# Two blocks of a feed-forward product pair by pair in single PSUM banks, their weights' parts made in an earlier stage

## The chip, the core and the metric

One core of a Trainium2 chip runs one launch of the kernel. The metric is the device time in microseconds. Five instruction streams work side by side and wait for each other by semaphores: TensorE (PE: matmuls and transposes), VectorE (DVE), ScalarE (ACT), GpSimd (POOL) and SyncE (SP), which here only issues DMAs. ScalarE issues DMAs too, in its own stream of instructions.

## What is computed

One layer of a diffusion backbone over 1152 tokens (1024 latent, 128 context) of width 1024, with a feed-forward width of 4096. The part after the token mixers is what the change touches:

```python
attn = _merge_heads(attend(_heads(q), k, v)) @ w_attn_proj
conv = (bg * _short_conv(cg * u, conv_w, conv_b)) @ w_conv_proj
mix = (jax.nn.sigmoid(ga) * attn + jax.nn.sigmoid(gc) * conv) @ w_o
x = _layer_norm(ALPHA * x + g1 * mix, ln1_g, ln1_b)
h = x * (1 + sc2) + sh2
f = jnp.square(jax.nn.relu(h @ w1 + b1)) @ w2 + b2
x = _layer_norm(ALPHA * x + g2 * f, ln2_g, ln2_b)
```

All is float32. An operand of a matmul is split into a high part (a cast) and a low part (the difference), and a product is three matmuls: high by high, high by low and low by high.

## The kernel before

The stages follow one another on TensorE: loading and modulation to 42 us of the span, attention to 380, the **mixers' stage** (gates, projections, convolution) to 758, the **output projection** by `w_o` to 887, the **first feed-forward product** to about 1300, the second to 1640, and the last layer norm.

*Mixers' stage.* Weights come through a `ring`: a raw tile `wr` by a DMA from SP (L94), `wh` as a cast on ScalarE (L109), `wl` as a difference on VectorE (L122). A chunk of 384 tokens takes one of six PSUM banks in turn. After each chunk `background(1)` takes one entry from the queue `bg`, which `gemv_rest` has filled with 109 entries: the rest of the modulation's product, VectorE's L741 on tiles `wmb`, in the pool `gp`.

*Output projection.* It runs in three passes, over 6, 9 and 3 pairs of a token tile and a half of the channels, 24 matmuls of 128x512 each (L1251 to L1253, tile `ps` in banks 4 to 7). A pass begins with the split of its own four weight tiles, which the code calls for during the last token tile of the pass before. Between matmuls `spend` hands out work from the list `todo`, by a budget in estimated us: the sums and moments of LN1 (`ln1_sum`, L985 to L989), its scaling (`ln1_apply`, L976 to L978 and L997 on `xk`), the *turns* (four transposes each of an `xk`, L1051, evacuated by ScalarE to `q`, L1061), and `combine`, which makes of the `q` of one **pair** (576 tokens, two times 288) the seven operands of a seven-product scheme in the manner of Strassen: high parts by ScalarE (L1069), low parts by VectorE (L1079), sums by VectorE (L1083). When `todo` is empty `spend` takes from `spare`: the two lists of `w1_ahead`. For each of the blocks 0 and 1 they load four raw tiles (L1150, `eh`), form the seven parts of the block's weights (sums L1134 in `S`, high L1158 in `ehT`, low L1162) and store them to DRAM as `w1d` (L1166 on SP), 14 units of two 128x512 tiles.

*First product.* There are 16 blocks `j`, each of seven products per pair, each product of 12 matmuls 128x288 (L1312 to L1314). Accumulators `dX`, `dV`, `dZ`, `dW` are two-bank tiles, one bank for each pair. Blocks 1 to 15 do both pairs at each product. Block 0 does all seven products of pair 0, then those of pair 1. During its first half the banks of pair 1 and the two of `dW` serve as four banks for the ten last turns, and during its second half `combine(1)` makes pair 1's operands; a product of pair 1 waits in the code until its part is made (`made <= k`). ScalarE copies accumulators out (`keep`, L1363), VectorE adds (`plus`, L1366); ReLU and square (L1320, L1321), differences (L1324), high and low parts (L1376, L1377) follow through the list `late`, and nine tiles per block go to DRAM by ScalarE's DMA issues (L1327, L1378, L1379). The weights' parts come from `w1d` by SP (L1191) for blocks 0 and 1, and are made in place (L1196, L1197) from block 2 on.

Of the kernel before, what the change touches and what calls it, by code (L numbers as in the profile page):

```python
# [144 lines left out]
def emit(nc, tc, ctx, aps, outs):  # L145
# [551 lines left out]
    gp = pool_on(s3, "gp", side="right")  # L697
# [16 lines left out]
    def gemv_rest():  # L714
# [3 lines left out]
        for g in range(8):  # L718
            st = {}

# [8 lines left out]
            def step(g=g, k=0, st=st):  # L729
                if k == 0:  # L730
                    start(g, st)
                    load(g, 0, st)
                if k + 1 < KB:
                    load(g, k + 1, st)
# [20 lines left out]
            def total(cond, g=g, st=st):  # L755
# [6 lines left out]
                dma(modd[cond:cond + 1, g * 512:(g + 1) * 512], ro)  # L762

# [26 lines left out]
        bg.append(fold)  # L790

# [29 lines left out]
    def attn_gate(j):  # L821
        w = ring.take()
        sg = tp.tile([P, NTOK + 4], F32, tag="t", name=f"sga{j}")
        for c in range(NCH):
            b = next_bank()
            run(chunk_mm(b, w, c))
            act(sg[:, csl(c)], b[:, :CH], AF.Sigmoid)
            background(1)
        sgs[j] = sg

    def attn_proj(j):
# [4 lines left out]
        for c in range(NCH):  # L836
# [3 lines left out]
            background(1)  # L840
# [52 lines left out]
    for j in range(6):  # L893
        w = ring.take()
        sg = tp.tile([P, NTOK + 4], F32, tag="t", name=f"sgc{j}")
        for c in range(NCH):
# [3 lines left out]
            background(1)  # L900
        w = ring.take(ahead=1 if j < 5 else 2)
        for c in range(NCH):
# [3 lines left out]
            background(1)  # L906
# [29 lines left out]

    HALVES = (slice(0, 512), slice(512, 1024))
# [4 lines left out]
    rawp = pool_on(sw, "rawp", side="right")  # L942
    wop = pool_on(swo, "wop", side="right")
    xkp = pool_on(sxk, "xkp", side="right")
    lnp = pool_on(sln, "lnp", side="right")
    tmp_n = [0]

    def tmp(pool, shape, tag, bufs, dtype=F32):
        tmp_n[0] += 1
        return pool.tile(shape, dtype, tag=tag, name=f"{tag}{tmp_n[0]}", bufs=bufs)  # L950

# [152 lines left out]
    WPARTS = ("A11", "S1", "S2", "A12", "S3", "S4", "A22")  # L1104
    NJ = NF // 2
    w1raw, w1sum, w1part = {}, {}, {}
    wtile = {}
# [8 lines left out]
    def w1_sum(u):  # L1116

        j, k = divmod(u, 7)
        if j >= NJ or (j, k) in w1sum:
            return  # L1120
        w1_load(j)
        a11, a12, a21, a22 = w1raw[j]
        name = WPARTS[k]
        if name[0] == "A":
            w1sum[j, k] = {"A11": a11, "A12": a12, "A22": a22}[name]
            return
        if name == "S4":
            t = w1sum[j, 2]
        else:
            t = tmp(wsp, [P, 512], "S1" if name == "S3" else name, 1)  # L1130
        w1sum[j, k] = t
        a, b, op = {"S1": (a21, a22, ALU.add), "S2": (w1sum.get((j, 1)), a11, ALU.subtract),
                    "S3": (a11, a21, ALU.subtract), "S4": (a12, w1sum.get((j, 2)), ALU.subtract)}[name]
        vec.tensor_tensor(out=t, in0=a, in1=b, op=op)  # L1134


    AHEAD = 2
    w1d = [dram.tile([P, 2, 512], F32, name=f"w1d{u}") for u in range(7 * AHEAD)]

    def ahead_tile(tag, dtype=F32):  # L1140
        tmp_n[0] += 1
        t = t1p.tile([P, 2, PT], dtype, tag=tag, name=f"e{tag}{tmp_n[0]}", bufs=1)
        return t.rearrange("p a b -> p (a b)")[:, :512]

    def w1_ahead(j):

        def load():
            w1raw[j] = [ahead_tile(f"h{n}") for n in ("11", "22", "12", "21")]
            for i in range(4):
                dma(w1raw[j][i], aps["w1"][j + i // 2 * NJ][:, HALVES[i % 2]])  # L1150

        st = {}

        def high(u):
            w1_sum(u)
            st[u] = (ahead_tile("hT2" if u % 2 else "hT4", F32R),
                     ahead_tile("hT3", F32R) if u % 2 else tmp(wsp, [P, 512], "lo2", 1, F32R))
            nc.scalar.copy(st[u][0], w1sum[j, u % 7])  # L1158

        def low(u):  # L1160
            hi, lo = st[u]
            vec.tensor_tensor(out=lo, in0=w1sum[j, u % 7], in1=f32(hi), op=ALU.subtract)  # L1162

        def keep(u):
            for i, x in enumerate(st.pop(u)):
                dma(w1d[u][:, i], f32(x))  # L1166

        out = [(0.0, load), (2.0, lambda: None)]
        units = range(7 * j, 7 * j + 7)
        for u in units:  # L1170
            out.append((0.0 if WPARTS[u % 7][0] == "A" else 0.7, lambda u=u: high(u)))
            if u > units[0]:
                out.append((0.0, lambda u=u: keep(u - 1)))
            out.append((1.6, lambda u=u: low(u)))
        out.append((1.0, lambda: keep(units[-1])))
        return out

    def w1_prep(u):
        j, k = divmod(u, 7)
        if j >= NJ:  # L1180
            return
        if u // 2 not in wtile:
            if u // 2 == 3:
                wtile[u // 2] = wo_last(u)
            else:
                wtile[u // 2] = [ringp.tile([P, 1024], F32R, tag=t, name=f"w1{t}{u}", bufs=3) for t in ("whi", "wlo")]
        hi, lo = (t[:, HALVES[u % 2]] for t in wtile[u // 2])
        w1part[u] = hi, lo
# [3 lines left out]
        else:  # L1192
            w1_sum(u)
            w1_sum(u + 1)
# [3 lines left out]
        if k == 6 and j + 1 >= AHEAD:  # L1198
            w1_load(j + 1)
# [20 lines left out]
    todo, spare = deque(), deque()  # L1220
# [13 lines left out]

    for j in range(AHEAD):
        spare.extend(w1_ahead(j))
# [44 lines left out]
    while spare:  # L1281
        spare.popleft()[1]()
# [4 lines left out]
    sln.close()  # L1287
    st0, sx1 = ExitStack(), ExitStack()
    t0p = pool_on(st0, "t0p")
    sp.close()  # L1290
# [3 lines left out]
    ps1 = pool_on(sp1, "ps1", space=bass.MemoryType.PSUM)  # L1294
# [5 lines left out]
    def dbank(tag, j):  # L1300
        return ps1.tile([P, 2, 512], F32, tag=tag, name=f"d{tag}{j}", bufs=1)

    def w1_mm(b, u, name, first, pairs):

        hi, lo = w1part[u]
        for p in pairs:
            o = b[:, p, :PT]
# [8 lines left out]
    def ht(tag, j):  # L1316
        return (t0p if tag[0] == "c" else t1p).tile([P, 2, PT], F32, tag=tag, name=f"{tag}_{j}", bufs=1)
# [8 lines left out]
    def spill(name, j, t):  # L1326
        nc.scalar.dma_start(hd[name, j], t)  # L1327

# [7 lines left out]
    both_p = slice(0, 2)  # L1336
    hip = None
# [17 lines left out]
    for j in range(NJ):  # L1355
        u = 7 * j
        bias = [b1c[:, j + i * NJ:j + i * NJ + 1] for i in range(2)]
        c1, c5, c2, c3 = (ht(t, j) for t in ("c1", "c5", "c2", "c3"))
        h = {n: ht("h" + n, j) for n in ("11", "22", "12", "21", "T2", "T3", "T4")}
        B = {}  # L1360

        def keep(out, b, f, sl=both_p):
            act(out[:, sl], b[:, sl, :PT], AF.Identity, bias=bias[f])  # L1363

        def plus(out, b, kept, sl=both_p):
            vec.tensor_tensor(out=out[:, sl], in0=b[:, sl, :PT], in1=kept[:, sl], op=ALU.add)  # L1366

        def finish(h=h, j=j):
            spill("T3", j, h["T3"])
            spill("T1", j, h["12"])  # L1370
            spill("T2", j, h["T2"])
            diff(h["T4"], h["21"], h["T2"])

            def parts(name, t):
                hi = tmp(hip, [P, 2, PT], "hi" + name, 1, F32R)
                nc.scalar.copy(hi, t)  # L1376
                vec.tensor_tensor(out=t.bitcast(F32R), in0=t, in1=f32(hi), op=ALU.subtract)  # L1377
                late.append(lambda: (nc.scalar.dma_start(hd[name, j][:, :, 0], f32(hi)),  # L1378
                                     nc.scalar.dma_start(hd[name, j][:, :, 1], t)))  # L1379
# [3 lines left out]


        for pairs in ((0,), (1,)) if j == 0 else ((0, 1),):
            sl = slice(pairs[0], pairs[-1] + 1)
            if pairs == (0,):
                store = list(segments(act_tiles(2), 0))
                todo.append((0.0, second_pair))
                B["X"], B["V"], B["W"] = dbank("X", 0), dbank("V", 0), dbank("W", "turn")  # L1390
                turn_banks.clear()
                turn_banks.extend(lambda n=n, i=i: B[n][:, i] for n, i in (("X", 1), ("V", 1), ("W", 0), ("W", 1)))
            for k, name in enumerate(WPARTS):
                new = {0: "X", 1: "V", 3: "Z", 6: "W"}.get(k)
                if new and pairs[0] == 0 and (j or k > 1):
                    while j == 0 and k == 6 and not made:
                        todo.popleft()[1]()
                    B[new] = dbank(new, j)
                if j:
                    w1_prep(u + k + 4)  # L1400
                while pairs == (1,) and made <= k:
                    todo.popleft()[1]()
                b = B["XVXZXVW"[k]]
                w1_mm(b, u + k, PARTS[k], bool(new), pairs)
                if k == 0:
                    keep(c1, b, 0, sl)
# [469 lines left out]
```

## Time and profile before

| | |
|---|---|
| time, median of 3 runs | 1688.82 us (1688.13 to 1691.61) |
| the profiled execution's own time | 1685.68 us |
| its span | 1683.9 us |
| PE, DVE, ACT, POOL busy | 95%, 61%, 43%, 12% |
| granted TensorE clock over the span | 0.979 |

The profiled execution is 3.1 us below the median, and its span 1.8 us below its own time. Shares are of the whole span; TensorE's missing 5% lies at the start and end, and between 758 and 953 us. In the page's 40 slices the granted clock, in tenths of full speed, reads `PEclk 9999999999999999999997899999999999999998`: it is short of 9 in two neighbouring slices in the middle (884 to 968 us) and in the last. In rows of the trace, "[1.49 <-ACT wh L109]" means that the engine stood idle for 1.49 us before the instruction and that ScalarE's line 109 writing `wh` released it. `SPq` and `ACTq` are the issues of DMAs, which don't count as busy time.

### The profile page before, as it was taken

How to read it: one execution, taken by the hardware profiler on the slowest of the kernel's cores; microseconds unless marked ns; L12 is line 12 of the kernel's file. 1: busy time of each engine (PE TensorE's matmuls, PEld its weight loads, DVE VectorE, ACT ScalarE, POOL GpSimd, SP SyncE). 2: the span in 40 equal slices, each digit the busy share in tenths (PEclk: the TensorE clock that was granted, in tenths of full speed). 3: DMA queues.
4: the chain of work that ended last, by engine and by line, in shares of the span. 5: the costliest groups of instructions: out<-in, count | busy, mean ns of one | idle time of the engine just before them, and what ended most of it. 6: DMA issues, size and time to landing. Idle time of an engine off the chain costs nothing.

```text
span 1683.9 us, 27308 instructions
## 1 busy us (share of the span) xinstructions
PE 1605.1 (95%) x10432; PEld 1543.4 (92%) x10432; DVE 1027.2 (61%) x1777; ACT 730.4 (43%) x1384; POOL 200.2 (12%) x214
## 2 busy tenths in 40 slices
PE   7999999999999999998886899999999999999995
PEld 5799999999999999996765799999999999999995
DVE  6568888654555565245563566666666457875666
ACT  5367777511122111132455465555655435454030
POOL 2145555100000001110000000000000121000002
PEclk9999999999999999999997899999999999999998
DMA  8332221222222222217534444454557898777792
GB/s 323 130 95 67 71 50 51 76 97 92 94 89 65 80 88 88 45 51 243 181 101 162 163 148 166 156 177 165 170 170 269 278 331 277 232 252 243 231 328 89
DMA packets 151819, 260.28 MB, mean 155 GB/s; under 512 B 40656, under 2 KB 58704, under 8 KB 151688
## 3 DMA queue, kind: packets, MB, share of 16 engines
q1 hardware_dynamic: 121320, 211.34, 38.9%
q10 hardware_dynamic: 30368, 47.20, 7.8%
q8 instruction: 82, 1.34, 0.3%
q14 instruction: 49, 0.40, 0.1%
HBM read 191.60 MB, written 66.88 MB: 154 GB/s over the span
## 4 chain that ended last, share of the span: by engine, by line
PE 77%; DVE 9%; ACT 6%; issue 3%; DMA 3%; POOL 0%; SPq 0%; POOLq 0%; ACTq 0%; DVEq 0%
PE ps L363 8%; PE ps L365 8%; PE ps L361 8%; PE pq L1565 6%; PE pq L1566 6%; PE pq L1567 6%; PE dX L1312 3%; PE dX L1314 3%; PE dX L1313 3%; PE ps L813 2%; PE ps L812 2%; PE ps L811 2%; PE dV L1313 2%; PE dV L1312 2%; PE dV L1314 2%
## 5 line engine op out<-in xcount | busy, mean ns | idle before, releaser
L365 PE MATMUL ps<-ahi,wl 128*128 128x384 f32 x864 | 292.5, 339 | 0.0
L361 PE MATMUL ps<-ahi,wh 128*128 128x384 f32 x864 | 292.5, 339 | 0.0
L363 PE MATMUL ps<-alo,wh 128*128 128x384 f32 x864 | 292.5, 339 | 0.0
L1565 PE MATMUL pq<-xh,vh 128*128 128x288 f32 x640 | 189.7, 296 | 4.5 <-ACT accc L1661 2.4
L1566 PE MATMUL pq<-xl,vh 128*128 128x288 f32 x640 | 188.8, 295 | 0.0
L1567 PE MATMUL pq<-xh,vl 128*128 128x288 f32 x640 | 188.2, 294 | 0.0
L361 PEld LDWEIGHTS ps<-ahi,wh 128*128 128x128 f32 x864 | 162.4, 188 | 1.5 <-issue 0.3
L363 PEld LDWEIGHTS ps<-alo,wh 128*128 128x128 f32 x864 | 162.5, 188 | 0.8
L365 PEld LDWEIGHTS ps<-ahi,wl 128*128 128x128 f32 x864 | 162.4, 188 | 0.0
L1565 PEld LDWEIGHTS pq<-xh,vh 128*128 128x128 f32 x640 | 119.9, 187 | 5.2 <-ACT accc L1661 2.6
L1567 PEld LDWEIGHTS pq<-xh,vl 128*128 128x128 f32 x640 | 120.6, 188 | 0.0
L1566 PEld LDWEIGHTS pq<-xl,vh 128*128 128x128 f32 x640 | 120.1, 188 | 0.0
L1532 DVE TENSOR_TENSOR xl<-hraw,xh 128x576 fp32r<-128x576 f32 x80 | 60.5, 756 | 78.3 <-ACT xh L1528 78.2
L122 DVE TENSOR_TENSOR wl<-wr,wh 128x1024 fp32r<-128x1024 f32 (+1 forms) x54 | 61.2, 1137 | 62.9 <-ACT wh L109 62.8
L741 DVE SCALAR_TENSOR_TENSOR acc<-wmb,sil,acc 128x512 f32<-128x512 f32 x112 | 81.6, 774 | 28.9 <-DMA wmb<-wmb 28.9
L1713 POOL TENSOR_TENSOR xm<-xm,ag 128x1024 f32<-128x1024 f32 x9 | 22.3, 2481 | 625.9 <-DMA xm<-xd 587.6
L1528 ACT CAST xh<-hraw 128x576 fp32r<-128x576 f32 x80 | 53.9, 673 | 97.5 <-issue 40.8
L1312 PE MATMUL dX<-hxahi,w1whi 128*128 128x288 f32 x248 | 74.6, 301 | 7.1 <-ACT q L1061 4.2
L1314 PE MATMUL dX<-hxahi,w1wlo 128*128 128x288 f32 x248 | 74.1, 299 | 0.1
L563 ACT ACTIVATE s<-s,st 128x512 f32<-128x512 f32 (+1 forms) x72 | 49.6, 688 | 51.5 <-DVE st L561 50.9
L1363 ACT ACTIVATE c<-dX,b1c 128x576 f32<-128x576 f32 (+1 forms) x51 | 36.4, 713 | 74.7 <-PE dX L1314 70.5
L109 ACT CAST wh<-wr 128x1024 fp32r<-128x1024 f32 (+1 forms) x62 | 57.7, 949 | 20.0 <-DMA wr<-wo 11.4
(354 smaller groups left out, 4377.2 us busy)
## 6 DMA issues: line engine op xcount, KB each, us to landing
w2r<-w SPq DMA_DIRECT2D x144, 256.0 KB
hraw<-hdT SPq DMA_DIRECT2D x60, 288.0 KB
wmb<-wmb SPq DMA_DIRECT2D x64, 256.0 KB
w1r<-w SPq DMA_DIRECT2D x28, 512.0 KB
hdB<-h ACTq DMA_DIRECT2D x48, 288.0 KB
hdT<-hT ACTq DMA_DIRECT2D x48, 288.0 KB
hraw<-hdB SPq DMA_DIRECT2D x44, 288.0 KB
mr<-wma SPq DMA_DIRECT2D x16, 512.0 KB
```

The lines of the kernel that those rows point to most:

```text
L122: engine.tensor_tensor(out=lo[:, :w], in0=self.raw.pop(i)[:, :w], in1=hi.bitcast(F32)[:, :w], op=ALU.subtract)
L361: mm(b[:, :CH], lhsT=hi[:, ws], rhs=a[0][:, kb, :], start=first and kb == 0, stop=False)
L363: mm(b[:, :CH], lhsT=hi[:, ws], rhs=a[1][:, kb, :], start=False, stop=False)
L365: mm(b[:, :CH], lhsT=lo[:, ws], rhs=a[0][:, kb, :], start=False, stop=last and kb == n - 1)
L741: vec.scalar_tensor_tensor(out=a, in0=t, scalar=sil[:, k, cond:cond + 1], in1=a, op0=ALU.mult, op1=ALU.add)
L1312: mm(o, lhsT=hi[:, ws], rhs=xh, start=first and kb == 0, stop=False, **kw)
L1313: mm(o, lhsT=hi[:, ws], rhs=xl, start=False, stop=False, **kw)
L1314: mm(o, lhsT=lo[:, ws], rhs=xh, start=False, stop=kb == 3, **kw)
L1532: vec.tensor_tensor(out=xl, in0=f32(x), in1=f32(xh), op=ALU.subtract)
L1565: mm(o, lhsT=hi[:, ws], rhs=xh[:, i], start=j == 0, stop=False)
L1566: mm(o, lhsT=hi[:, ws], rhs=xl[:, i], start=False, stop=False)
L1567: mm(o, lhsT=lo[:, ws], rhs=xh[:, i], start=False, stop=j == NJ - 1)
```

## The change

The making of the 14 units moves from the output projection to the mixers' stage: `w1_ahead` becomes the last entry of `bg`, opens a pool of its own (one buffer each for high, low, the four raw tiles and the sums) when the modulation's pool has been closed, and appends its 33 entries. `background(1)` becomes `background(1 + c % 2)`, four entries for three chunks, so that 142 entries find 156 places instead of 109 finding 117. The modulation's loads `wmb` are issued one further ahead. `spare` is gone, and `spend` deals only from `todo`.

In the first product both blocks 0 and 1 go pair by pair, in the order (0, pair 0), (1, pair 0), (0, pair 1), (1, pair 1), in single banks 0 to 3 of the pool that the output projection used. The turns use banks 6 and 7, two instead of four. Blocks 2 to 15 take two-bank tiles as before; their pool opens at block 2. The parts of blocks 0 and 1 are loaded from `w1d` twice, once for each pair. `keep`, `plus`, ReLU, square, differences, casts and stores of the two blocks work on one pair (128x288) instead of two (128x576). SP's DMA issues rise from 735 to 763, ScalarE's instructions from 1405 to 1447, VectorE's from 1703 to 1719; TensorE's stay at 10086.

```diff
@@ gemv_rest
         bg.append(fold)
+        bg.append(w1_ahead)
@@ new, before the mixers' loops
+    def w1_ahead():
+        sgp.close()
+        prep = pool_on(s3, "prep", side="right")
+        st = {}
+
+        def load(j):
+            w1raw[j] = [tmp(prep, [P, 512], f"r{i}", 1) for i in range(4)]
+            for i in range(4):
+                dma(w1raw[j][i], aps["w1"][j + i // 2 * NJ][:, HALVES[i % 2]])
+
+        def high(u):
+            if st:
+                keep(u - 1)
+            w1_sum(u, prep)
+            st[u] = tmp(prep, [P, 512], "hi", 1, F32R), tmp(prep, [P, 512], "lo", 1, F32R)
+            nc.scalar.copy(st[u][0], w1sum[u // 7, u % 7])
+
+        def low(u):
+            hi, lo = st[u]
+            vec.tensor_tensor(out=lo, in0=w1sum[u // 7, u % 7], in1=f32(hi), op=ALU.subtract)
+
+        def keep(u):
+            for i, x in enumerate(st.pop(u)):
+                dma(w1d[u][:, i], f32(x))
+
+        for j in range(AHEAD):
+            bg.append(lambda j=j: load(j))
+            for u in range(7 * j, 7 * j + 7):
+                bg.extend([lambda u=u: high(u), lambda u=u: low(u)])
+            bg.append(lambda: keep(max(st)))
@@ attn_gate, attn_proj, and the convolution's loops
-            background(1)
+            background(1 + c % 2)
@@ output projection
+    BLOCKS = [(j, (p,)) for p in range(2) for j in range(AHEAD)] + [(j, (0, 1)) for j in range(AHEAD, NJ)]
...
-        while todo and (room[0] >= 0 or not todo[0][0]) or spare and room[0] >= 0:
-            cost, fn = (todo or spare).popleft()
+        while todo and (room[0] >= 0 or not todo[0][0]):
+            cost, fn = todo.popleft()
...
-    for j in range(AHEAD):
-        spare.extend(w1_ahead(j))
@@ first product
-    sp.close()
+    turn_banks.clear()
+    turn_banks.extend(lambda i=i: bank(i) for i in (6, 7))
...
-    def dbank(tag, j):
+    def dbank(tag, j, pairs):
+
+        if len(pairs) == 1:
+            return bank("XVZW".index(tag)).rearrange("p (a b) -> p a b", a=1)
         return ps1.tile([P, 2, 512], F32, tag=tag, name=f"d{tag}{j}", bufs=1)
...
+    for n, (j, pairs) in enumerate(BLOCKS):
+        sl = slice(pairs[0], pairs[-1] + 1)
...
+            w1_prep(s_ + 4)
+            while pairs[-1] == 1 and made <= k and todo:
+                todo.popleft()[1]()
...
-                    spend(1.6)
+            if todo:
+                spend(1.3)
+            do_late()
```

On ScalarE, at the boundary between the first and the second pass of the output projection, the order before is this (`ehT` is a high part of `w1_ahead`, `wh` that of `w_o`'s tiles, `bag` the moments of LN1):

```order
L1158 CAST ehT_7974<-eh_7817 128x512
L1158 CAST ehT_8028<-eh_8011 128x512
L109 CAST wh_8041<-wr_7802 128x1024
L109 CAST wh_8053<-wr_7806 128x1024
L109 CAST wh_8065<-wr_8045 128x1024
L109 CAST wh3o_8082<-wr_8057 128x1024
L1158 CAST ehT_8119<-S_8117 128x512
L976 ACT_TABLE_LOAD
```

and of the changed kernel this:

```order
L109 CAST wh_7916<-wr_7788 128x1024
L109 CAST wh3o_7914<-wr_7820 128x1024
L109 CAST wh_8095<-wr_7920 128x1024
L109 CAST wh_8107<-wr_7924 128x1024
L109 CAST wh_8119<-wr_8099 128x1024
L109 CAST wh3o_8131<-wr_8111 128x1024
L1037 ACT_TABLE_LOAD
```

The casts of `w_o` follow each other with none of `w1_ahead` among them. On TensorE, where the seventh product of (block 0, pair 0) ends, stands before the first product of pair 1, on `hxahi_8882`, a part that `combine(1)` makes:

```order
L1313 MATMUL dW_9088<-hxs_8446,wh_8900 128x288
L1314 MATMUL dW_9088<-hxs_8445,wl_8901 128x288
L1312 MATMUL dX_8884<-hxahi_8882,w1whi_8687 128x288
L1313 MATMUL dX_8884<-hxahi_8882,w1whi_8687 128x288
L1314 MATMUL dX_8884<-hxahi_8882,w1wlo_8688 128x288
```

and in the changed kernel the first product of (block 1, pair 0), on `hxahi_8451`, the part of pair 0 that block 0 began with:

```order
L1313 MATMUL ps_9109<-hxs_8458,w1whi_8940 128x288
L1314 MATMUL ps_9109<-hxs_8457,w1wlo_8941 128x288
L1312 MATMUL ps_9142<-hxahi_8451,w1whi_8940 128x288
L1313 MATMUL ps_9142<-hxahi_8451,w1whi_8940 128x288
L1314 MATMUL ps_9142<-hxahi_8451,w1wlo_8941 128x288
```

Pair 1's first product has moved behind the 84 matmuls of (block 1, pair 0). On ScalarE in the mixers' stage, convolution gates (`sgc` is a gate's sigmoid, `hi` a high part of `w1_ahead`), the order before is

```order
L109 CAST wh_6904<-wr_6743 128x1024
L109 CAST wh_6965<-wr_6811 128x512
L899 ACTIVATE sgc_6971<-ps_6972 128x384
L899 ACTIVATE sgc_6971<-ps_7000 128x384
L203 CAST acch_0_7026<-acc_6781 128x512
L899 ACTIVATE sgc_6971<-ps_7030 128x384
```

and in the changed kernel

```order
L845 CAST hi_7060<-S_7058 128x512
L109 CAST wh_7063<-wr_6901 128x512
L968 ACTIVATE sgc_7069<-ps_7070 128x384
L968 ACTIVATE sgc_7069<-ps_7097 128x384
L845 CAST hi_7126<-S_6993 128x512
L968 ACTIVATE sgc_7069<-ps_7130 128x384
L845 CAST hi_7158<-r_6874 128x512
L109 CAST wh_7161<-wr_7002 128x1024
```

The 14 casts `hi` stand between the gates' sigmoids and the splits of the ring's weights.

## Rows read from the trace of the kernel before

**Rows 1.** Windows: stretch, length, busy PE, PEld, DVE, ACT, POOL, clock, DMA share, GB/s

```profile
380.00:760.00 380.00, 379.66 (x2178) 375.05 (x2177) 190.40 (x295) 81.42 (x139) 28.86 (x36) 1.00 0.25 78
890.00:929.00 39.00, 27.36 (x126) 25.46 (x126) 9.30 (x15) 22.93 (x59) 0.00 (x0) 0.65 0.36 137
```

**Rows 2.** Timeline, TensorE, second pass boundary: start, us, work, [idle before <-releaser]

```profile
797.97 0.49 PE L1251 MATMUL ps<-wh,ahi 128*128 128x512 f32 x1 [1.49 <-ACT wh L109]
799.23 0.80 PE L1252 MATMUL ps<-wl,ahi 128*128 128x512 f32 x1 [0.76 <-DVE wl L122]
800.25 0.63 PE L1251 MATMUL ps<-wh,ahi 128*128 128x512 f32 x1
803.88 0.49 PE L1251 MATMUL ps<-wh,ahi 128*128 128x512 f32 x1 [0.36 <-ACT wh L109]
805.14 0.50 PE L1252 MATMUL ps<-wl,ahi 128*128 128x512 f32 x1 [0.77 <-DVE wl L122]
808.32 0.50 PE L1252 MATMUL ps<-wl3o,ahi 128*128 128x512 f32 x1 [1.52 <-DVE wl3o L122]
```

**Rows 3.** Timelines of ScalarE and SyncE's queue around the same boundary

```profile
789.09 0.62 ACT L1158 CAST ehT<-eh 128x512 fp32r<-128x512 f32 x1 [0.94 <-DMA w1d<-ehT]
796.35 0.62 ACT L1158 CAST ehT<-eh 128x512 fp32r<-128x512 f32 x1 [6.64 <-DMA eh<-w]
796.88 1.99 ACT L109 CAST wh<-wr 128x1024 fp32r<-128x1024 f32 x2
786.15 0.32 SPq L1166 DMA_DIRECT2D w1d<-ehT  x1
```

**Rows 4.** Timelines of TensorE and VectorE, second pass: turns that wait

```profile
839.60 0.66 PE L1051 MATMUL ps<-ident,xk 128*128 128x128 f32 x4 [1.79 <-ACT xk L997]
847.01 0.66 PE L1051 MATMUL ps<-ident,xk 128*128 128x128 f32 x4 [0.80 <-ACT xk L997]
834.87 0.69 DVE L1162 TENSOR_TENSOR ehT<-S,ehT 128x512 fp32r<-128x512 f32 x1 [4.28 <-ACT ehT L1158]
```

**Rows 5.** Timeline, TensorE: end of output projection, blocks 0 and 1

```profile
886.61 0.39 PE L1253 MATMUL ps<-wh3o,alo 128*128 128x512 f32 x1
889.56 0.37 PE L1312 MATMUL dX<-hxahi,w1whi 128*128 128x288 f32 x1 [2.56 <-DMA w1whi<-w1d]
952.96 0.29 PE L1312 MATMUL dX<-hxahi,wh 128*128 128x288 f32 x1
974.91 0.29 PE L1312 MATMUL dW<-hxs,w1whi 128*128 128x288 f32 x1
```

**Rows 6.** TensorE's waits, 887 to 953: us in total, times, longest

```profile
PE dWturn L1051 <- ACT q L1061: 5.7, 2, 3.5
PE dX L1312 <- ACT q L1061: 4.2, 2, 2.1
```

**Rows 7.** Window of L1061 alone (turns' evacuations): busy of ACT, clock, DMA

```profile
887.00:953.00 66.00, 16.10 (x48) 0.72 0.39 136
```

**Rows 8.** Window of L1069 alone (casts of combined parts): busy of ACT, clock, DMA

```profile
887.00:953.00 66.00, 9.30 (x10) 0.72 0.39 136
```

**Rows 9.** Window of L997 alone (LN1's scaling): busy of ACT, clock, DMA

```profile
887.00:953.00 66.00, 2.69 (x4) 0.72 0.39 136
```

**Rows 10.** Groups by shape, ScalarE, 740 to 1320: busy us, mean ns, idle

```profile
L1363 ACT ACTIVATE c<-dX,b1c 128x576 f32<-128x576 f32 x45 | 33.4, 742 | 62.0 <-PE dX L1314 57.8 <-DMA hdB<-h 3.9
L1363 ACT ACTIVATE c<-dX,b1c 128x288 f32<-128x288 f32 x6 | 3.0, 497 | 12.7 <-PE dX L1314 12.7
```

**Rows 11.** ScalarE's queue, one issue of a store

```profile
947.98 0.34 ACTq L1327 DMA_DIRECT2D hdB<-h  x1
```

**Rows 12.** DMA, 885 to 960: GB/s in 40 slices

```profile
GB/s 204 199 317 404 399 392 401 393 391 319 17 0 0 0 0 0 0 0 0 0 9 0 0 0 0 44 312 203 155 303 106 0 0 0 157 189 205 349 412 131
```

**Rows 13.** Page: DMA queues (packets, MB, share of 16 engines)

```profile
q1 hardware_dynamic: 121320, 211.34, 38.9%
q10 hardware_dynamic: 30368, 47.20, 7.8%
```

More of the change, by code (lines that the diff above doesn't have):

```diff
@@ L717, in gemv_rest @@
         nc.scalar.copy(ones_r, ones)
-        for g in range(8):
-            st = {}
+        sts = [{} for _ in range(8)]
+        for g, st in enumerate(sts):
             def start(g=g, st=st):
@@ L762, in total @@
                 dma(modd[cond:cond + 1, g * 512:(g + 1) * 512], ro)
+                if cond and g + 1 < 8:
+                    load(g + 1, 0, sts[g + 1])
+                    load(g + 1, 1, sts[g + 1])
             for k in range(KB):
@@ L1137, in emit @@
[L1137 to L1188, printed above, removed]
+        j, k = BLOCKS[s_ // 7][0], s_ % 7
+        u = 7 * j + k
+        if s_ // 2 not in wtile:
+            wtile[s_ // 2] = [ringp.tile([P, 1024], F32R, tag=t, name=f"w1{t}{s_}", bufs=3) for t in ("whi", "wlo")]
@@ L1189, in w1_prep @@
+        hi, lo = (t[:, HALVES[s_ % 2]] for t in wtile[s_ // 2])
+        w1part[s_] = hi, lo
         if j < AHEAD:
@@ L1218, in emit @@
     seen, sums = {}, 0
[L1220 removed]
+    todo = deque()
     room = [0.0]
@@ L1353, in second_pair @@
             todo.extend(closures + [(0.0, count)])
-    for j in range(NJ):
-        u = 7 * j
-        bias = [b1c[:, j + i * NJ:j + i * NJ + 1] for i in range(2)]
[L1358 to L1371, printed above, removed]
+    store = list(segments(act_tiles(2), 0))
@@ new lines, in sums @@
+        def sums(h=h):
+            square(h["21"])
+            diff(h["T3"], h["22"], h["12"])
+            diff(h["12"], h["12"], h["11"])
+            diff(h["T2"], h["22"], h["12"])
+        for k in range(7):
+            s_ = 7 * n + k
+            new = {0: "X", 1: "V", 3: "Z", 6: "W"}.get(k)
+            if new:
+                B[new] = dbank(new, n, pairs)
+            w1_prep(s_ + 4)
+            while pairs[-1] == 1 and made <= k and todo:
+                todo.popleft()[1]()
+            b = B["XVXZXVW"[k]]
+            w1_mm(b, s_, PARTS[k], bool(new), pairs)
+            if k == 0:
+                keep(c1, b, 0)
+            elif k == 1:
+                keep(c5, b, 1)
+            elif k == 2:
+                keep(c2, b, 0)
+            elif k == 3:
+                plus(h["11"], b, c1)
+            elif k == 4:
+                keep(c3, b, 1)
+                plus(h["22"], b, c5)
+            elif k == 5:
+                plus(h["12"], b, c2)
+            elif not last:
+                plus(h["21"], b, c3)
+            if last and k == 6:
+                break
+            if todo:
+                spend(1.3)
+            do_late()
+            if k == 3:
+                after(lambda h=h: square(h["11"]))
+            elif k == 4:
+                after(lambda h=h, spill=spill: (square(h["22"]), spill("B11", h["11"])))
+            elif k == 5:
+                after(lambda h=h, spill=spill: (square(h["12"]), spill("B22", h["22"])))
+            elif k == 6:
+                after(sums)
+                after(lambda f=finish: late.append(f))
@@ L1577, in emit @@
     ps2 = pool_on(sp2, "ps2", space=bass.MemoryType.PSUM)
-    after(lambda h=h, j=j: (square(h["21"]), diff(h["T3"], h["22"], h["12"]), diff(h["12"], h["12"], h["11"]),
-                            diff(h["T2"], h["22"], h["12"])))
+    after(sums)
     after(finish)
@@ L1723, in emit @@
         if n == 8:
-            for stack in (swo, sw, st1):
+            for stack in (sw, st1):
                 stack.close()
```

187 lines of the change are left out of this document (73 added, 114 removed).

## The prediction

> **What bounds the kernel now.** I read first the table of stretches. In the mixers' stage TensorE is busy 379.66 of 380 us at full clock, with VectorE half idle and ScalarE four fifths idle [rows 1]: whatever small work goes there is hidden as long as it holds nobody up. From 758 us on it is different. [...] The timeline gives the frame: the output projection ends at 886.61 + 0.39 = 887.0 (call it T), block 0 begins at 889.56, block 1 at 952.96, and block 1's last four or so matmuls stand at 974.91 [rows 5]. So the two blocks end at about 975.3 = T + 88.3. Block 1, both pairs, takes 22.3 us, 168 matmuls at 0.133 us: two blocks without a hindrance are 44.7 us. Block 0's 63.4 us are the loss. [...]
>
> **Removing `w1_ahead` from the output projection.** The second pass begins late: idle 1.49 + 0.76 + 0.36 + 0.77 + 1.52 = 4.9 us, and behind the first two stand eight matmuls of 0.63 us [rows 2], where the usual one takes 0.39 [rows 5]: 8 x 0.24 = 1.9. Sum 6.8 us. The cause is one row up the chain: ScalarE's cast `ehT` at 796.35 waited 6.64 us for a load of `w1_ahead`, and `wh` stood behind it to 796.88 [rows 3]. In the new order nothing stands before these casts, so they begin when their buffers are free, some 4 to 5 us earlier. The third and fourth weight tile still come through two raw buffers, so the last wait of 1.5 and about another 1.5 stay: gain 3.8 (bounds 2 and 5). Two turns waited 1.79 + 0.80 for LN1's scaling [rows 4]; LN1 stood on VectorE behind a low part of `w1_ahead` that had itself waited 4.28 us [rows 4]. With that gone I take the whole 2.6 (bounds 0 and 2.6). The third pass begins with waits that LN1 and `combine(0)` cause on VectorE, not `w1_ahead`; their order changes by a few rows there, and I take nothing (bounds -1.5 and +1.5). Together T comes 6.4 us earlier (bounds 0.5 and 9).
>
> **Putting it into the mixers' stage.** 14 casts on ScalarE, 14 lows and 8 sums on VectorE, 8 loads and 28 stores on SP, some 14 x 0.62 + 22 x 0.69 = 24 us of work on two engines beside 380 us with at least 190 idle [rows 1]. It costs nothing as work. As a chain it could cost: there is one buffer for the high part, so a cast waits for the store before. A store was issued at 786.15 and let the next cast of its buffer go at 789.09 [rows 3], 2.9 us. One unit is then cast 0.62 + store 2.9 = 3.5 us, low parts likewise, while two entries of the queue come round in 1.5 chunks, 4.7 us at the mean of a gate's chunk (24 matmuls) and a projection's (12) at the stage's pace. Behind a late cast stand on ScalarE the gates' sigmoids and the ring's `wh`, and TensorE waits for those only when six banks are full. SP's loads of the ring stand behind stores that wait for a low part, with a whole weight tile of lead. I take 0. The bounds are 0 and 14 x 2.9 = 41 us, if every store held TensorE by its whole length; the value near 0 is nearest to the row of the stage itself, where VectorE's 190 us of similar entries left 0.34 us of idle TensorE.
>
> **The two blocks pair by pair.** The matmuls are the same. What changes is who waits. Before, pair 1's operands had to be made in the 39 us of pair 0's only half-block, and PE stood for the turns. Now 84 more matmuls of pair 0 lie between, and nobody but a turn needs pair 1 until (0, pair 1). So I ask how much ScalarE has to do between T and the end of the four half-blocks, because everything passes through it:
> - the ten turns' evacuations, 16.1 us [rows 7];
> - the casts of combined parts, 9.3 [rows 8], and LN1's last two scalings with their moments, 2.7 + 0.3 = 3.0 [rows 9];
> - a half-block's own work, 4 `keep`, 8 ReLU and square, 2 casts, at 0.497 us each at this width [rows 10]: 7.0, times four 27.8, less the 10 instructions of the last one that run beside block 2 (5.0): 22.8;
> - 9 stores for each of three half-blocks, 27 issues at 0.34 [rows 11], which the busy share hides: 9.2;
> - four casts of block 2's weights at 0.62 [rows 3]: 2.5.
>
> Sum 62.9 us. TensorE needs 44.7 and ten turns of 0.66 [rows 4], 51.3. ScalarE is the longer one. It won't run without a gap, since turns and accumulators still pass to and fro. Before, it was busy 22.93 of the 39 us [rows 1], 16 us of gaps; now TensorE always has a half-block of work that doesn't need ScalarE's newest result, but the turns have two banks instead of four. I take half, 8: the four half-blocks end at T + 71, bounds T + 63 and T + 79. Against T + 88.3 the gain is 17.3 (bounds 9 and 25). The first wait, 2.56 us for `w1whi` [rows 5], is inside T + 88.3, and I let it stand inside T + 71 as well.
>
> The rows show what the narrower work costs: `keep` takes 0.497 us at 288 and 0.742 at 576 [rows 10], so two halves cost 0.25 more than a whole, on 24 more instructions 6 us, and 18 more issues another 6, all of it in the sum above. [...]
>
> **Transfers.** 28 units of two 128x512 tiles are 14.7 MB, twice as much as before; with 1.75 blocks of stores (9 x 288 x 1024 bytes each, 4.6 MB), `xd` (1.6) and block 2's raw weights (1.0) it is 21.9 MB in some 70 us. Between 890 and 902 the trace shows 392 to 404 GB/s [rows 12]; at 400 that is 55 us. It is hidden, but not by much.
>
> **The sum.** 6.4 + 17.3 = 23.7 us. From the profiled execution's 1685.7 that is 1662; the median of the runs is 3.1 above that execution, so 1665. From block 2 on nothing changes. With all bounds together the forecast's own range is 1655 to 1679.
>
> **Rivals.**
> - *TensorE becomes the bound* (chance 0.09). If ScalarE's half-block work slips behind into block 2, where ScalarE has room, the end is TensorE's 51.3 + 1.5 = T + 53: gain 35 + 6.4, time 1647. For it: all of it but `keep` is put off by design. Against it: each of the ten turns and the parts of pair 1 are ScalarE's too, 28 us with LN1 before (0, pair 1) can run, and a full queue does not look ahead.
> - *The transfers set the pace* (0.17). SP's queue as a whole moves 211.34 MB in 38.9% of the span, 323 GB/s, and ScalarE's 47.20 MB in 7.8%, 359 [rows 13]. If ScalarE's issues wait for their places, the stores' 4.6 MB / 359 = 12.8 us come on top of its 71: T + 84, gain 4.3 + 6.4, time 1678. A sign of it is there already: `keep` waited once 3.9 us for `hdB<-h` [rows 10]. Against it: 21.9 MB at 323 are 68 us, still under 71. [...]
> - *The chain of stores stalls the mixers' stage* (0.08). One buffer, so each of 14 casts holds the sigmoids and `wh` behind it on ScalarE in front of a TensorE that is now never idle. It decides against the change from 24 us on, 1.7 of the 2.9 us of each unit: at 41 us the time is 1665 + 41 = 1706. Half of this (0.04) is slower, most of the rest within what can't be told. For it: in the output projection this same chain cost 6.64 us once. Against it: six banks of lead, and 3.5 us against 4.7.
>
> **How the numbers follow.** The forecast has 0.66. A measurement of this kernel tells about 0.2%, 3.4 us, from no change. Faster: 0.66 + 0.09 + 0.17 + 0.01 = 0.93; the same 0.03, slower 0.04. The range shall hold 8 in 10: forecast and transfers together have 0.83, so it reaches from below the forecast's fast end, 1652, to 1681, past the transfers' time; TensorE's 1647 and the stalled mixers lie outside.
>
> **What would show it.** Right: 380 to 758 us stays at 100% TensorE at full clock; the second pass begins with less than 3.5 us of idle time and no row of 0.63; no row of the mixers' stage waits for ScalarE; the four half-blocks end at T + 63 to T + 79 with ScalarE's queue, issues included, nearly without gaps, and the waits inside them are on `q`, `hxs` and on accumulators that `keep` has not freed. Wrong: idle TensorE before 758 behind `hi` or a sigmoid; waits of TensorE on `w1whi<-w1d`, or of ScalarE on `hd`, in the half-blocks (transfers); waits on `q` as long as before (the turns' two banks, which I have priced inside the 8 us of gaps); block 2 later than full speed because it inherits the last half-block's work.

## The result

| | before | after |
|---|---|---|
| median | 1689.72 us (4 runs) | 1670.72 us (4 runs, 1667.97 to 1671.68) |
| ratio, 95% interval | | 0.9884 [0.9867, 0.9902] |
| span of the profiled execution | 1683.9 us | 1669.9 us |

The changed kernel is 19 us faster (16.6 to 22.5 by the interval), and inside the range of the prediction, which said 1665. The two profiled executions differ by 14.0 us only: that of before is 4.0 below its median, that of after 1.0 above. What follows is read from these two and adds up to 14.

### The profile page after: what moved, and what is told of

It is laid out like the page before. It is cut to its first block, busy times and chain, and to the rows that moved or that the text cites. A ratio compares the mean times of both kernels' runs of the same rounds, so it can differ in the third digit from the quotient of the medians.

```text
span 1669.9 us, 27468 instructions
## 1 busy us (share of the span) xinstructions
PE 1599.8 (96%) x10432; PEld 1539.7 (92%) x10432; DVE 1026.0 (61%) x1793; ACT 734.8 (44%) x1408; POOL 201.4 (12%) x214
## 4 chain that ended last, share of the span: by engine, by line
PE 77%; DVE 8%; DMA 5%; ACT 5%; issue 3%; SPq 1%; POOL 0%; ACTq 0%; POOLq 0%; DVEq 0%
PE ps L363 8%; PE ps L365 8%; PE ps L361 7%; PE pq L1552 6%; PE pq L1553 6%; PE pq L1554 6%; PE dX L1312 3%; PE dX L1314 3%; PE dX L1313 3%; PE dV L1312 2%; PE dV L1314 2%; PE dV L1313 2%; PE ps L880 2%; PE ps L881 2%; PE ps L882 2%
## 5 line engine op out<-in xcount | busy, mean ns | idle before, releaser
L1699 POOL TENSOR_TENSOR xm<-xm,ag 128x1024 f32<-128x1024 f32 x9 | 22.5, 2497 | 607.6 <-DMA w2r<-w 545.0
L743 DVE SCALAR_TENSOR_TENSOR acc<-wmb,sil,acc 128x512 f32<-128x512 f32 x112 | 78.2, 748 | 12.3 <-DMA wmb<-wmb 12.2
L1312 PE MATMUL dX<-hxahi,w1whi 128*128 128x288 f32 x224 | 67.5, 301 | 5.5 <-DVE h L1367 5.5
L1314 PE MATMUL dX<-hxahi,w1wlo 128*128 128x288 f32 x224 | 67.0, 299 | 0.0
L881 PE MATMUL ps<-acl,wh 128*128 128x384 f32 x192 | 64.2, 334 | 0.0
```

Of the source, the lines that this page charges most:

```text
L881: mm(b[:, :CH], lhsT=hi[:, ws], rhs=parts[kb][1][:, cs_], start=False, stop=False)
L1312: mm(o, lhsT=hi[:, ws], rhs=xh, start=first and kb == 0, stop=False, **kw)
L1314: mm(o, lhsT=lo[:, ws], rhs=xh, start=False, stop=kb == 3, **kw)
```

## The profile after

T again is the end of the output projection. The stretches of the changed kernel, to be laid beside [rows 1] (columns as there):

```profile
380.00:760.00 380.00, 378.56 (x2173) 374.14 (x2172) 193.47 (x307) 85.49 (x145) 27.80 (x34) 1.00 0.33 101
881.00:920.00 39.00, 29.95 (x174) 28.00 (x172) 16.60 (x25) 31.12 (x76) 0.00 (x0) 0.82 0.63 216
920.00:940.00 20.00, 15.96 (x116) 15.34 (x115) 12.84 (x19) 9.63 (x19) 0.00 (x0) 1.00 0.99 330
940.00:953.00 13.00, 12.69 (x92) 11.99 (x90) 4.03 (x9) 5.90 (x14) 0.00 (x0) 1.00 1.02 360
953.00:962.00 9.00, 3.55 (x15) 3.55 (x16) 6.83 (x13) 5.82 (x12) 0.00 (x0) 0.74 0.24 85
```

The mixers' stage still looks full, but 380 us hold 1.4 us of idle TensorE where there were 0.3. At the start of the first product ScalarE is busy 31.12 of 39 us, where it was 22.93, and TensorE's mean clock is 0.82 where it was 0.65 (this stretch begins at T, that of before 3 us behind its T). From 920 to 953 the DMA engines are full: a share of 0.99 to 1.02 at 330 to 360 GB/s. And in 953 to 962 TensorE has only 3.55 us of work in 9.

The boundaries of the output projection's second and third pass, in TensorE's timeline:

```profile
804.27 0.50 PE L1248 MATMUL ps<-wh,ahi 128*128 128x512 f32 x1 [0.23 <-ACT wh L109]
805.53 0.50 PE L1249 MATMUL ps<-wl,ahi 128*128 128x512 f32 x1 [0.76 <-DVE wl L122]
807.73 0.50 PE L1249 MATMUL ps<-wl3o,ahi 128*128 128x512 f32 x1 [0.54 <-DVE wl3o L122]
...
859.47 0.50 PE L1248 MATMUL ps<-wh,ahi 128*128 128x512 f32 x1 [1.75 <-ACT wh L109]
860.73 0.50 PE L1249 MATMUL ps<-wl,ahi 128*128 128x512 f32 x1 [0.76 <-DVE wl L122]
865.46 0.50 PE L1248 MATMUL ps<-wh,ahi 128*128 128x512 f32 x1 [0.46 <-ACT wh L109]
```

The first three rows are the second pass, to be laid beside [rows 2]: its first two waits are gone, 0.23 + 0.76 + 0.54 = 1.5 us remain of 4.9, and no matmul of 0.63 us stands there any more. The last three are the third pass. Its wait for `wl` is 0.76, where the kernel before had

```profile
866.62 0.80 PE L1252 MATMUL ps<-wl,ahi 128*128 128x512 f32 x1 [4.08 <-DVE wl L122]
```

but the wait for `wh` just before has grown from 0.85 to 1.75. From the last matmul of the second pass to T the third takes 24.1 us instead of 26.2.

The two blocks, same engine, as in [rows 5]: the last matmul of the output projection, the first of the first product, the last of the four half-blocks and the first of block 2.

```profile
881.02 0.40 PE L1250 MATMUL ps<-wh3o,alo 128*128 128x512 f32 x1
881.26 0.29 PE L1312 MATMUL ps<-hxahi,w1whi 128*128 128x288 f32 x1
...
952.68 0.29 PE L1314 MATMUL ps<-hxs,w1wlo 128*128 128x288 f32 x1
958.45 0.61 PE L1312 MATMUL dX<-hxahi,w1whi 128*128 128x288 f32 x1 [5.48 <-DVE h L1367]
958.86 0.44 PE L1313 MATMUL dX<-hxahi,w1whi 128*128 128x288 f32 x1
```

T is 881.42; the first product begins at once; the four half-blocks end at 952.8 = T + 71.4; block 2 begins only at 958.45, after 5.48 us of waiting, and then at the lower clock (0.24 us from one matmul to the next, 22 of the first 24). What it waits for is seen on the other engines, in one row of SP's queue, one of ScalarE and two of VectorE:

```profile
947.40 14.58 SPq L1173 DMA_DIRECT2D w1r<-w  x3
953.66 0.62 ACT L1195 CAST w1whi<-w1r 128x512 fp32r<-128x512 f32 x1 [3.53 <-DMA w1r<-w]
955.16 0.69 DVE L824 TENSOR_TENSOR S<-w1r 128x512 f32<-128x512 f32 x1 [4.54 <-DMA w1r<-w]
957.94 0.45 DVE L1367 TENSOR_TENSOR h<-ps,c 128x288 f32<-128x288 f32 x1
```

The loads of block 2's raw weights `w1r` are issued from 947.4 on, behind the second round of `w1d` loads; ScalarE and VectorE wait 3.53 and 4.54 us for them, and the additions (L1367) that empty the last half-block's banks stand on VectorE behind the weights' sums (L824). So `dX`, which takes two of those banks, waits for an addition whose product had long been finished (the last matmul of all four half-blocks ended at 952.97, the addition began at 957.94).

Where the 14.0 us of the two spans come from, by TensorE's timeline. Its marks are the first 128x384 matmul of the attention ("start" below), the first of the output projection, T, and the first of blocks 2 and 3. The start, which the change doesn't touch, lies between 83.4 and 85.1 in all twelve profiles and is 0.8 us later here:

| stage | before | after | gain |
|---|---|---|---|
| start of attention | 83.4 | 84.3 | -0.8 |
| from there to the output projection | 674.6 | 678.6 | -4.0 |
| output projection | 128.9 | 118.5 | +10.4 |
| T to the end of the two blocks | 88.3 | 71.4 | +16.9 |
| block 2, beyond 22.4 us | 0.0 | 8.2 | -8.2 |
| the rest | | | -0.3 |

## The experiments

On two chips, with the kernel before beside them each time (medians 1687.6 to 1688.4): e5 to e8 on one, the others on another. e5, e6 and e7 ran once each, so they have no interval. "Half-blocks to" is the time from T to the end of the four half-blocks, and to block 2's first matmul where TensorE waited between the two; for the kernel before and e3_only_ahead it is that of blocks 0 and 1. "Both stages" is the time from the output projection's first matmul to the same end. Both are read from one profile of each kernel.

| kernel | us | ratio [95%] | half-blocks to | both stages |
|---|---|---|---|---|
| before | 1687.6 to 1688.4 | | T + 88.3 | 217.2 |
| r_after | 1671.25 | 0.9893 [0.9876, 0.9909] | T + 69.2, block 2 at T + 75.3 | 189.7 |
| e3_only_ahead | 1671.01 | 0.9900 [0.9886, 0.9915] | T + 76.3 | 196.8 |
| e4_only_blocks | 1680.15 | 0.9953 [0.9936, 0.9969] | T + 74.1, block 2 at T + 79.6 | 204.0 |
| e1_early_raw | 1664.37 | 0.9856 [0.9840, 0.9872] | T + 69.4 | 190.0 |
| e2_pace | 1667.21 | 0.9877 [0.9859, 0.9896] | T + 72.8, block 2 at T + 78.4 | 191.3 |
| e8_both | 1660.37 | 0.9831 [0.9817, 0.9844] | T + 70.6 | 191.2 |
| e9_pool_stores | 1658.11 | 0.9815 [0.9801, 0.9830] | T + 66.5 | 187.0 |
| e5_no_square | 1661.82 | | T + 71.2 | 188.6 |
| e6_half_loads | 1661.13 | | T + 64.7 | 185.4 |
| e7_four_banks | 1661.15 | | T + 68.7 | 187.8 |

**The changed kernel beside the others.** Same file, on the chip of e1 to e4 and e9.

> The changed kernel again, on the chip of the other experiments: 0.986 to 0.991 of the kernel before, so that e1_early_raw's 0.9856 and e8_both's 0.9831 stand against a value measured beside them.

0.9893, where the first measurement had 0.9884; its output projection took 120.5 us and its half-blocks T + 69.2, where the profile above has 118.5 and T + 71.4. The two trade some 2 us from one execution to the next, so a difference of that size in one stage says nothing. Their sum trades less: 189.9 above, and 189.7 to 191.3 in the table for the four kernels that should hardly differ there (r_after, e1_early_raw, e2_pace, e8_both).

**Each half alone.** First half: the 14 units in the mixers' stage, blocks as before (the loops of the first product, the four turn banks and the order of block 0 are those of the kernel before).

```diff
+        bg.append(w1_ahead)
...
-            background(1)
+            background(1 + c % 2)
...
-        while todo and (room[0] >= 0 or not todo[0][0]) or spare and room[0] >= 0:
+        while todo and (room[0] >= 0 or not todo[0][0]):
```

> The kernel before (1689.7 us) with only the first half of the change: the 14 units are made in the mixers' stage, the blocks of the first product stay as they were. Theory: the mixers' stage gives back about 4 us, the output projection gains about 10.5, the first wait of 2.56 us on w1whi goes: in sum 7 to 9, 1681 to 1683, and the first product from its first matmul on takes the 399 us of before. Rival: the output projection's gain at its third pass (about 2.6) belongs to the other half of the change: 1683 to 1686.

More than either expectation: 0.9900, 17 us, nearly all of the whole change. The mixers' stage lost its 3 to 4 us, as said; the output projection took 120.5 us, 8.5 less, where 10.5 were expected. What was not foreseen is the first product:

```profile
881.55 0.40 PE L1249 MATMUL ps<-wh3o,alo 128*128 128x512 f32 x1
881.78 0.29 PE L1306 MATMUL dX<-hxahi,w1whi 128*128 128x288 f32 x1
...
958.27 0.29 PE L1306 MATMUL dX<-hxahi,w1whi 128*128 128x288 f32 x1
```

881.95 to 958.27 are 76.3 us for blocks 0 and 1 in their old order, 12.0 less than in the kernel before. The rows account for most of it: the first wait (2.56) is gone; TensorE's waits in the two blocks sum to 16.6 us instead of 21.9, that one included; some 52 matmuls instead of 99 run at the lower clock, 47 x 0.11 = 5.2 us. One unit of `w1_ahead` had been left for the end of the output projection (before: a cast on ScalarE at 888.08, its lows and stores behind it), ahead of the last tile's LN1, and with it the last turns came 2.5 us later after T. That this small delay and the lower clock explain all 12 us was argued from rows, not tried apart.

Second half alone: the order of half-blocks, the units made in the output projection.

```diff
+    for j in range(AHEAD):
+        spare.extend(w1_ahead(j))
...
-        bg.append(w1_ahead)
...
-            background(1 + c % 2)
+            background(1)
```

> The changed kernel with only its second half: two blocks pair by pair, and the 14 units made in the output projection as before. Theory: the halves are independent, so this one gains what the first product gained, 8 to 10 us: 1680 to 1682; the output projection takes its 129 us. Rival: the units' stores, the second loads and the half-blocks' stores meet after the output projection and the half-blocks get longer than T + 77: 1684 to 1688.

1680.15, 7.5 us: the theory's time. The output projection takes 129.9 us, the half-blocks end at T + 74.1 and block 2 waits as in the changed kernel. The two halves alone give 17 and 8 us, the whole change 17 to 19: they are not independent, since both shorten the same stretch behind T. On top of the first half the second shows nothing in the time: 1671.01 without it, 1671.25 with it. The half-blocks end 5 to 7 us sooner with it, and block 2's wait and lower clock take that back.

**Block 2's raw weights loaded earlier.**

```diff
             w1_prep(s_ + 4)
+            if s_ == 7:
+                w1_load(AHEAD)
```

> The changed kernel (1670.7 us), with block 2's two raw weight tiles loaded when (block 1, pair 0) begins instead of late in (block 1, pair 1). Theory: the 5.48 us for which TensorE waited at block 2's first matmul, and the 22 matmuls at the lower clock behind it (some 2.5 us), come from these loads standing behind the second round of w1d loads: the wait is under 1 us and the time 1662 to 1664. Rival: the wait is the handing over of single banks to two-bank tiles, which needs the last half-block's additions whatever the loads do: the wait stays above 4 us and the time within 1669 to 1672.

```profile
883.26 0.40 PE L1250 MATMUL ps<-wh3o,alo 128*128 128x512 f32 x1
...
953.09 0.29 PE L1312 MATMUL dX<-hxahi,w1whi 128*128 128x288 f32 x1
```

No wait at block 2's first matmul, at 953.09 = T + 69.4, and it runs at full clock (0.29); 1664.37, 6.9 us below the changed kernel on the same chip and 0.4 above the theory's 1662 to 1664. With the weights there, the banks' handing over shows no wait.

**A total no longer in the call of its cut.** Among the modulation's entries in the queue, a *cut* splits a sum of VectorE into high and low part (`acch`, `accl`), and the *total* behind it adds them up over the partitions by two matmuls of TensorE. A cut now returns `True` and ends the call:

```diff
+        owed[0] += n
+        while owed[0] > 0 and (bg or later):
+            owed[0] -= 1
+            if (bg or later).popleft()():
+                break
...
                 st["hl"] = hi, lo
+                return True
```

> The changed kernel, where a call of the mixers' background queue ends after a cut, so that the total which needs it comes one chunk later; what is left of the call is made up at the next. Theory: the 4 us that the mixers' stage lost come from totals of the modulation right behind their cut (waits of 1.08, 0.34 and 1.01 us), not from the chain of stores: the waits on acch and accl are under 0.5 us in sum, and the time is 2 to 3 us shorter, 1668. Rival: the 14 units' casts and stores cost the 4 us: no change, 1670 to 1672.

TensorE's waits from 320 us to the output projection, first of the changed kernel, then of this one:

```profile
PE ps L761 <- DVE accl L204: 1.4, 2, 1.0
PE ps L760 <- ACT acch L203: 1.1, 1, 1.1
PE ps L365 <- DVE wl L122: 0.9, 2, 0.5
```

```profile
PE ps L365 <- DVE wl L122: 0.2, 1, 0.2
```

The waits on the modulation's totals are gone, the output projection begins at 758.0 instead of 762.9 (0.8 of that is the earlier start of the attention), and the median is 4.0 us below r_after's. The intervals of the two ratios overlap, so the time alone wouldn't decide; the stage does. From the start of the attention to the output projection it takes 674.6 us here, 674.8 in e8_both and 674.7 in e9_pool_stores, which have the same edit, as in the kernel before (674.6), and 677.4 to 678.6 in the seven profiles with the units there and without the edit. The chain of stores never reached TensorE: before seven of the 14 casts ScalarE stood idle until a store `w1d<-hi` had landed, 23.1 us in sum, but from 650 us on, where `w1_ahead` has its places, no TensorE row of the changed kernel waits.

**Both together.**

> e1_early_raw and e2_pace together. Theory: two losses in different stages add: 1664.4 - 3 = 1661, a ratio of 0.983 to 0.985 to the kernel before.

1660.37, ratio 0.9831, against 1664.4 - 4.0 = 1660.4: they add.

**What sets the length of the half-blocks.** e1_early_raw without ReLU and square of blocks 0 and 1 (so that part of the activations is left out):

```diff
+        sq = square if n >= 2 * AHEAD else lambda t: None
```

> e1_early_raw, where its four half-blocks end at T + 69.4 (T is the end of the output projection). ReLU and square of blocks 0 and 1 are left out, some 26 ScalarE instructions of 0.45 us before that point, 12 us. Theory: ScalarE sets the length of the half-blocks, so they end at T + 58 to T + 62. Rival: turns, TensorE and the transfers set it: T + 67 or more.

```profile
879.29 0.40 PE L1250 MATMUL ps<-wh3o,alo 128*128 128x512 f32 x1
...
950.91 0.29 PE L1312 MATMUL dX<-hxahi,w1whi 128*128 128x288 f32 x1
```

950.91 - 879.69 = 71.2: not a microsecond shorter, and 1.4 us by both stages, where the theory wanted 7 to 11. The theory that ScalarE's work is the bound falls. The second round of loads halved (the low parts of pair 1's weights are not read):

```diff
-            for i, x in enumerate((hi, lo)):
+            for i, x in enumerate((hi, lo) if s_ < 7 * AHEAD else (hi,)):
...
+            if s_ >= 7 * AHEAD:
+                w1part[s_] = hi, hi
```

> e1_early_raw, where the second round of w1d loads, for pair 1, brings only the high parts (the low operand of these products is the high part again): 3.7 MB less, some 9 us of transfers. Theory (ScalarE is the bound, the transfers add waits only in the third and fourth half-block): the ScalarE waits on landings of w1d there go, the half-blocks end at T + 65 to T + 68. Rival (transfers set the pace): T + 61 to T + 64. If the transfers are hidden: T + 69.

```profile
882.00 0.40 PE L1252 MATMUL ps<-wh3o,alo 128*128 128x512 f32 x1
...
947.06 0.29 PE L1314 MATMUL dX<-hxahi,w1whi 128*128 128x288 f32 x1
```

947.06 - 882.40 = 64.7, 4.7 us less than e1_early_raw (4.6 by both stages), between the theory's span and the rival's. Four turn banks instead of two:

```diff
-    turn_banks.extend(lambda i=i: bank(i) for i in (6, 7))
+    turn_banks.extend(lambda i=i: bank(i) for i in (4, 5, 6, 7))
```

> e1_early_raw with four turn banks instead of two (4 to 7). Theory: the 3.8 us for which turns waited on ScalarE's evacuations are ScalarE's time in another place, so the half-blocks end within 1.5 us of T + 69.4. Rival: the two banks hold TensorE up: T + 65 to T + 67.

T + 68.7, within the 1.5 us (2.2 us less by both stages, in this one execution). So neither ScalarE's work nor, as far as one execution tells, the banks, but something with the transfers. The whole times of the three, 1661.1 to 1661.8, don't tell them apart. In the changed kernel's trace it is this: an issue of ScalarE's queue, its next instruction, and the matmul that waits for that one.

```profile
930.41 0.33 ACTq L1370 DMA_DIRECT2D hdB<-h  x1
930.78 0.50 ACT L1364 ACTIVATE c<-ps,b1c 128x288 f32<-128x288 f32 x1 [1.48 <-DMA w1wlo<-w1d]
931.33 0.40 PE L1312 MATMUL ps<-hxahi,w1whi 128*128 128x288 f32 x1 [2.90 <-ACT c L1364]
```

ScalarE does nothing from 929.3 to 930.4, because its next instruction is the issue of a store, and what lets it go is by the profile the landing of a load that SP had issued; `keep` stands behind, and TensorE waits 2.90 us for the bank. That gave a theory to try: the stores of the four half-blocks issued from GpSimd's queue, on top of e8_both.

```diff
+    st_q = nc.gpsimd
...
-            nc.scalar.dma_start(hd[name, j][:, sl], t)
...
+            (st_q if n_ < 2 * AHEAD else nc.scalar).dma_start(hd[name, j][:, sl], t)
...
+                q_ = st_q if n_ < 2 * AHEAD else nc.scalar
+                late.append(lambda: (q_.dma_start(hd[name, j][:, sl, 0], f32(hi)),
+                                     q_.dma_start(hd[name, j][:, sl, 1], t)))
```

> e8_both (1660.4 us; half-blocks to T + 70.6), with the stores of the four half-blocks issued from GpSimd's queue instead of ScalarE's; all else as it was. Theory: what stretches the half-blocks is not ScalarE's work (leaving 12 us of it out changed nothing) but that its issues of stores wait there for landings while keep and casts stand behind them. Then ScalarE's waits on DMA landings between T and T + 71 fall from some 10 us to under 2, the half-blocks end at T + 64 to T + 67, and the time is 1655 to 1658. Rival: the transfers themselves are the pace, whoever issues them: T + 69 to T + 72 and 1659 to 1662, with the waits moved to TensorE on w1d parts.

ScalarE's waits on landings in the half-blocks, of e8_both:

```profile
ACT hiB L1383 <- DMA w1wlo<-w1d: 3.6, 1, 3.6
ACT hiT L1383 <- DMA w1whi<-w1d: 3.2, 1, 3.2
ACT hiT L1383 <- DMA hdB<-hiB: 2.7, 1, 2.7
ACT c L1367 <- DMA w1wlo<-w1d: 1.4, 1, 1.4
```

and the largest of its waits, and the only one on a landing, of e9_pool_stores:

```profile
ACT c L1368 <- PE ps L1318: 8.9, 7, 3.0
ACT hxs L1133 <- DMA w1whi<-w1d: 1.0, 1, 1.0
```

From 3.6 + 3.2 + 2.7 + 1.4 = 10.9 us to 1.0; ScalarE now waits for TensorE. And TensorE's waits for `keep`, first of e8_both, then of e9_pool_stores:

```profile
PE ps L1315 <- ACT c L1367: 7.1, 3, 2.7
PE ps L1316 <- ACT c L1368: 3.0, 3, 2.6
```

The half-blocks:

```profile
879.13 0.40 PE L1254 MATMUL ps<-wh3o,alo 128*128 128x512 f32 x1
...
946.04 0.29 PE L1316 MATMUL dX<-hxahi,w1whi 128*128 128x288 f32 x1
```

946.04 - 879.53 = 66.5, inside the theory's 64 to 67, 4 us less than e8_both and as much as TensorE's waits for `keep` fell; 1658.11, at 0.9815 the fastest of all and 0.1 above the theory's 1655 to 1658, though its interval overlaps that of e8_both, which ran on the other chip. The waits go with the length in the other profiles too: ScalarE's on landings are 11.6 us in the changed kernel, 10.2 in e1_early_raw and 12.1 in e5_no_square, and 1.6 in e6_half_loads, where fewer bytes move.

The rival that the transfers themselves set the pace is not quite out, because the edit changed them as well. Rates from 880 to 952 us in 40 slices and the queue of the stores (packets, MB, share of 16 engines), first of e8_both, then of e9_pool_stores:

```profile
GB/s 273 351 401 363 294 193 8 133 363 384 262 33 1 238 295 336 355 361 355 240 279 350 262 333 354 386 324 311 340 269 216 293 382 328 285 310 394 352 113 31
q10 hardware_dynamic: 3922, 4.02, 16.0%
GB/s 279 364 404 385 364 44 7 264 397 321 186 5 102 264 339 364 338 404 332 223 187 384 379 369 363 404 390 411 405 404 412 400 386 399 363 45 82 82 86 379
q0 software_dynamic: 1484, 4.59, 16.5%
```

From 918 to 943 us the first moves 216 to 386 GB/s, the second 363 to 412: the stores, of tiles of the same size, go in packets of some 3.1 KB instead of 1.0, and SP's loads, which stood 5.3 us for landings of stores in e8_both, don't stand for one. That the 4 us come by way of ScalarE is shown by the waits; how much of them the moved issues gave, and how much the sooner landings, is not shown.

## Why the prediction was right, and where not

*The mixers' stage, 0 with bounds 0 and 41*: measured 4.0. The size is inside the bounds, and the rival that was named, the chain of stores, is not what cost it: it made ScalarE stand, but never TensorE. What the step left out is the second effect of `background(1 + c % 2)`: the modulation's own entries come faster too, and where a call takes two, a total follows its cut at once, with TensorE waiting 1.08, 0.34 and 1.01 us (the first two at 343 us, still beside the attention). I had costed the entries that came in, and not those already there whose pace changed.

*The output projection, 6.4, bounds 0.5 and 9*: measured 10.4 in one profile, outside the bounds, and 8.5 in the other. The second pass gave 4.9 + 1.9 - 1.5 = 5.3 at its start, 3.8 predicted: I had let 3 us of the waits stand, and 1.5 did. (Of the eight matmuls of 0.63 us, six take that in the trace, one 0.80 and one 0.44; the sum of 1.9 is the same.) The turns' 2.6 came as predicted. The third pass, taken at 0 within 1.5, gave 2.1: its 4.08 us were a `wl` that stood on VectorE behind `combine(0)` and a tile of LN1's sums, and with the units gone that work from `todo` runs earlier, so that `wl` follows its `wh` at once.

*The half-blocks, T + 71*: measured T + 71.4 and T + 69.2, and for a wrong reason; that the number fits is luck. The sum of ScalarE's work, 62.9, was no lower bound that mattered: with 12 us less of it the half-blocks ended at T + 71.2. The 8 us put down as gaps, half of the gaps before, were the term that counted, and they are waits of ScalarE for landings, 11.6 us in the changed kernel: the transfers' rival in another form. Its condition, that ScalarE's issues wait, came true at nearly its price (12.8), but not on top of the 71 (T + 84): the waits fill the time in which ScalarE's work was not the bound. The rate I took for the transfers, 400 GB/s, was that of 256 KB loads and stores on SP's queue; with stores of 144 KB on ScalarE's queue among the loads the trace shows 330 to 360 at a full share. The gain against T + 88.3 was also put down to the wrong part: 12 of the 17 us come already with `w1_ahead` out of the way (T + 76.3), and the order of half-blocks itself is worth 5 to 7, which block 2's wait takes back as long as its weights come late.

*"From block 2 on nothing changes"*: this is the step that failed. It cost 5.5 us of waiting and 2.7 of lower clock. I had counted the raw weights' megabyte among the transfers, and not asked where its load stands in SP's queue: behind all 56 loads of `w1d`, while the block that needs it begins right after them. The prediction's last sign of being wrong was a late block 2, for another cause.

*The sum*: 23.7 predicted; -0.8 - 4.0 + 10.4 + 16.9 - 8.2 = 14.3 in the profiles, 19 in the medians. In these profiles the errors of 4 us in the mixers' stage and in the output projection, of opposite sign, cancelled, which is luck too, and the handing over to block 2 is what is missing. The rows' 0.497 us against half of 0.742 [rows 10] is what the narrower tiles cost in `keep`; but where 12 us less of ScalarE's work shortened nothing (T + 71.2 against T + 69.4), the 6 us more that were counted for it are not likely to have cost much.

## What to carry to other kernels

When a background queue is given more work, ask what its faster pace does to the entries already in it: here a consumer right behind its producer turned hidden work into a stall (1.08, 0.34 and 1.01 us of TensorE). When a load is doubled, look for the load that stands behind it in the same queue and is needed right after (block 2 began 5.48 us late for its weights). And an engine that issues DMAs as well as computing is not described by its busy time: here its issues waited for landings, those of another queue too (10.9 us in e8_both), with its arithmetic behind them. Look at what holds the issues before counting instructions.

## What the runs showed of the hardware

In the changed kernel an issue of a store on ScalarE's queue was held, by the profile, until a load issued by SP had landed (1.48 us before `keep` at 930.78). In e8_both such waits sum to 10.9 us, 8.2 of them for loads of SP and 2.7 for a store of ScalarE's own queue; with the issues on GpSimd's queue 1.0 is left. Whether the engine or the program's order of semaphores asks for this, no run shows. With loads of 256 KB on SP's queue and stores of 144 KB on ScalarE's the DMA engines were full at 330 to 360 GB/s (the changed kernel from 920 to 953 us, a share of 0.99 to 1.02); with the same stores on GpSimd's queue, in packets of 3.1 KB instead of 1.0, the rate was 363 to 412 (e9_pool_stores from 918 to 943 us). Between 890 and 902 us the kernel before had moved 391 to 404 [rows 12], loads and some stores of 256 KB, all on SP's queue. Between 880 and 952 us the two queues of e8_both took 65.9% and 16.0% of the 16 engines' time, and its waits show beside it that the issuing engine itself was held, for the 10.9 us above.
